# A decoder block on one core: SyncE's queue gets an order written out by hand, and 32 of 192 modulation rows move to the output projection

## The chip, the core and the metric

The kernel runs on one core of a Trainium2 chip. The core has TensorE (matrix products into PSUM), VectorE, ScalarE, GpSimd and SyncE, which here only issues DMA transfers. Each engine works through its own instructions in their order; between engines, semaphores say what has been done. The metric is the device time of one execution in microseconds. The kernel before takes 2344.61 us, the median of three runs from 2343.13 to 2346.32.

## The reference

One block on 512 tokens of width 2048, everything in float32:

```python
mod = c_act @ w_ada[l] + b_ada[l]
sh1, sc1, gt1, sh2, sc2, gt2 = jnp.split(mod[:, None, :], N_MOD, axis=-1)
h = _rmsnorm(x, norm1_g[l]) * (1.0 + sc1) + sh1
p = h @ w_in[l]
y_rwkv = _rwkv7_mixer(p[..., :N_RWKV_COLS], ...)
y_pool = _pool_mixer(p[..., N_RWKV_COLS:], ...)
mix = jnp.concatenate([y_rwkv, y_pool], axis=-1) @ w_out[l]
x = x + gt1 * mix
h = _rmsnorm(x, norm2_g[l]) * (1.0 + sc2) + sh2
x = x + gt2 * _conv_ffn(h, w_up[l], conv_w[l], conv_b[l], w_down[l])
return _rmsnorm(x, norm_f_g)
```

`_rwkv7_mixer` is a recurrence with a 64 x 64 state for each of 16 heads; its inputs r, k and v are 1024 columns each of `p`, its decay and gates come from three small low-rank products. `_pool_mixer` takes causal means over 2, 4, 8 and 16 tokens and a 256 x 256 product for each. The MLP has 5632 columns twice, with a causal convolution of width 3.

## The kernel before

Activations are kept transposed: 128 channels by 512 tokens in a tile. A float32 product is made of three faster ones: weights and activations are split into a rounded part and its remainder (`split_weights`: a load into `wraw`, a cast to `whi` on ScalarE, a subtraction to `wlo` on VectorE; `mm3`: three matmuls). `wraw` has four buffers, `whi` and `wlo` three each.

The stages are: the first norm and the first eight column tiles of the input projection (up to 156 us in the profile); the *recurrence* (163 to 761), in which the other 27 column tiles (`win_units`, L333) are interleaved with the recurrence and the pools; the output projection (761 to about 950), of which the first eight output tiles are made in whole rows of 512 tokens and the other eight in two halves of 256; the MLP; the last norm.

The recurrence treats two heads at a time, eight *pairs*. `stage_a` of a pair loads r, k and v and a small matrix `lw`, makes decays and scores, stores the 16 x 16 triangles of the scores to DRAM and loads them back in another layout (`dn`, `nl`), inverts them on VectorE in 14 doubling steps (`prod`, `xyl`, L466 to L475), and passes the result through DRAM again (`dx`, `x4w`, `x4`). `stage_b` does the chunked state update, and `post` the norm, the bonus and the gate, and stores the tile to `mixd` in DRAM, from which the output projection loads it. r, k and v of pair p are three column tiles of the projection; `win_pair` spills them to DRAM (`sp`), and `stage_a` loads them from there. One more load in this stretch are the modulation rows: 48 columns of `mod` are products of `c_act` with rows of `w_ada`, done on VectorE (`ada_rest`, L343 to L352) with the row in quarters: 4 x 48 = 192 loads of 256 KB into `war` (three buffers), each with one multiplication that sums along the row. `cq` holds the quarter of `c_act`. The other modulation rows are made before and after.

The loop `recurrence()` writes TensorE's order out by hand. It keeps a clock of its own, in us: one matmul of the projection adds 0.23, and each step of a stage yields what it takes and how long its next step must wait. Whenever no step is ready, a matmul of the projection is put in. Every sixth of these a modulation row follows. Inside `manual_schedule` TensorE's instructions stand in the order in which the loop emits them. Those of the other engines, SyncE's loads and stores too, are ordered by a scheduler, by priority and by when it thinks them ready.

Of the kernel before, what the change touches and what calls it, by code (L numbers as in the profile page):

```python
# [1 line left out]

# [26 lines left out]
NB = 10  # L29
NJ = NF // 2  # L30
# [27 lines left out]
def block_kernel(ctx, tc, a, out, stop=None, dbg=None):  # L58
# [52 lines left out]
    def split_weights(src, eng=V):  # L111
        raw = wp.tile([P, WC], F32, tag="wraw", name="wraw", bufs=4)
        nc.sync.dma_start(raw, src)
        hi = wp.tile([P, WC], F32R, tag="whi", name="whi", bufs=3)
        S.copy(hi, raw)  # L115
        lo = wp.tile([P, WC], F32R, tag="wlo", name="wlo", bufs=3)
        eng.tensor_tensor(lo, raw, hi[:, :].bitcast(F32), op=ALU.subtract)  # L117
        return hi, lo
# [7 lines left out]
    def project(ps, src, acts, start=True, stop=True, engs=(V,)):  # L126

        n = len(acts)
        for k0 in range(0, n, WC // P):
            wh, wl = split_weights(src[:, k0 * P : k0 * P + WC], engs[k0 // 4 % len(engs)])  # L130
# [48 lines left out]
    if True:  # L179
# [28 lines left out]
        for k in range(KT):  # L208
# [14 lines left out]
            for i0 in range(0, 8, WC // P):  # L223
                wh, wl = split_weights(a["win0"][k, :, i0 * P : i0 * P + WC])
# [8 lines left out]
        if True:  # L233
# [13 lines left out]
            S.activation(xwa[0:64, :], xwa[0:64, :], AF.Tanh)  # L247
            xg1 = ra.tile([P, T], F32, tag="xg1", name="xg1")
# [15 lines left out]
            upad = [ring16("upad") for i in range(2)]  # L264
            for i in range(2):
                V.memset(upad[i][:, 0:16], 0.0)
                S.copy(upad[i][:, 16:], pf[6 + i])
            ps0ctx.close()

    def load_pw(gi):  # L270
        t = ra.tile([P, T], F32, tag="war", name="pw", bufs=3)
# [24 lines left out]
    def pool_back(gi, zs, pw):  # L296
        for d in range(2):
# [6 lines left out]
            if gi:  # L304
                nc.sync.dma_start(mixd[8 + j], mx)
# [16 lines left out]

    def win_units(fi, ps):
# [16 lines left out]
    cq = [None]  # L340
    modq = ra.tile([P, 4, 48], F32, tag="modq", name="modq")

    def ada_rest(n0, n1):  # L343
        for n in range(n0, n1):
            kq, j = divmod(n, 48)
            if j == 0:
                cq[0] = ra.tile([P, T], F32, tag="cq", name="cq")
                nc.sync.dma_start(cq[0], cact[0:1, kq * T : (kq + 1) * T].partition_broadcast(P))
            wa = ra.tile([P, T], F32, tag="war", name="war", bufs=3)
            nc.sync.dma_start(wa, a["ada2"][kq, j, :, :])  # L350
            V.scalar_tensor_tensor(wa, wa, 1.0, cq[0], op0=ALU.mult, op1=ALU.mult,  # L351
                                   accum_out=modq[:, kq, j : j + 1])  # L352
# [16 lines left out]
    class Pair:  # L369
        begun = False  # L370

# [9 lines left out]
    def stage_a(p, q):  # L381
# [14 lines left out]
        yield 0.0, 4.0  # L396
# [15 lines left out]
        mid = ra.tile([P, NL, 1], F32, tag="mid", name="mid", bufs=2)  # L412
# [40 lines left out]
        nl = ra.tile([64, 16, 16], F32, tag="nl", name="nl")  # L453
        dn = tc.dram_tile([64, 16, 16], F32, name=f"dn{p}")
        for b in range(8):
            nc.sync.dma_start(dn[8 * b : 8 * b + 8, :, :].rearrange("s i j -> i s j"),
                              nt[16 * b : 16 * b + 16, :, 16 * (b % 4) : 16 * (b % 4) + 16])
        nc.sync.dma_start(nl, dn[:, :, :])
# [5 lines left out]
        V.scalar_tensor_tensor(k2, r, col("rk", p), k2, op0=ALU.mult, op1=ALU.mult)  # L464
        xyl = ra.tile([64, 2, 16, 16], F32, tag="xyl", name="xyl")
        V.tensor_add(xyl[:, 1, :, :], nl, lanei)  # L466
        prod = ra.tile([64, 64], F32, tag="prod", name="prod")
# [9 lines left out]
        nc.sync.dma_start(dx[:, :, :, :], xyl)  # L477
        for b in range(8):
            nc.sync.dma_start(x4w[16 * b : 16 * b + 16, :, :, 16 * (b % 4) : 16 * (b % 4) + 16],
# [254 lines left out]
    with tc.manual_schedule(engines={mybir.EngineType.PE}):  # L734
        recurrence()
# [606 lines left out]
```

## Time and profile before

One profiled execution took 2349.0 us; its span, from the first instruction to the last, is 2347.1 us, and the mean granted clock of TensorE 0.981.

| stretch, us | what | TensorE busy, us | VectorE busy, us | granted clock |
|---|---|---|---|---|
| 163 to 636 | recurrence up to the last pair's `stage_a` | 415.55 of 473 | 355.05 | 0.95 |
| 636 to 761 | rest of the recurrence | 121.56 of 125 | 69.61 | 0.99 |
| 761 to 852 | output projection, whole rows | 90.79 of 91 | 42.27 | 1.00 |
| 852 to 950 | output projection, half rows | 93.85 of 98 | 65.19 | 0.98 |

In rows of waits the first name is the engine and line that waited and the second what ended the wait; then total us, times and the longest. In rows of groups, the count, the busy us and mean ns of one, and the idle time of the engine before them. `SPq` is SyncE's queue. A row of transfers gives the count, the size and the median us from issue to landing.

### The profile page before, as it was taken

The page shows a single profiled execution, that of the slowest core. Times are in us where ns is not written, and L with a number is a line of the kernel's source. Part 1 is how long each engine was busy: PE and PEld are TensorE (multiplying, and loading weights), DVE is VectorE, ACT ScalarE, POOL GpSimd, SP SyncE. Part 2 cuts the span into 40 slices and gives each one's busy share as a digit, 9 for nine tenths or more (in the row PEclk, how much of TensorE's full clock was granted, in tenths as well). Part 3 has the DMA queues.
Part 4 walks back from the last instruction along what each step waited for, and adds up shares of the span by engine and source line. Part 5 has one row for each costly group of instructions (what it writes and reads, how often), then busy time and mean ns, then how long its engine had stood idle before and what let it go on. Part 6 is the DMA issues. An engine that isn't in the chain of part 4 may idle for free.

```text
span 2347.1 us, 42629 instructions
## 1 busy us (share of the span) xinstructions
PE 2206.0 (94%) x17090; PEld 1958.5 (83%) x17090; DVE 1611.8 (69%) x2543; ACT 1006.5 (43%) x1416; POOL 126.1 (5%) x183
## 2 busy tenths in 40 slices
PE   4778798898899999999999999999999999999997
PEld 3656566666677799999999999999999888888897
DVE  7977786877665366788888877777777645353454
ACT  3243333333333346655555555555555422233353
POOL 0000000000000010111010100000000000110000
PEclk9999899999999999999999999999999999999998
DMA  9966665666533766698888877777776667663464
GB/s 353 339 221 187 210 198 168 202 201 186 151 77 93 251 187 184 204 271 235 250 225 248 234 200 201 199 199 197 200 197 196 221 222 268 226 211 112 124 189 155
DMA packets 200218, 480.77 MB, mean 205 GB/s; under 512 B 46481, under 2 KB 53201, under 8 KB 191825
## 3 DMA queue, kind: packets, MB, share of 16 engines
q1 hardware_dynamic: 180098, 410.91, 53.7%
q0 software_dynamic: 18864, 66.07, 13.7%
q8 instruction: 134, 2.20, 0.4%
q10 hardware_dynamic: 1056, 1.05, 0.1%
q14 instruction: 66, 0.54, 0.1%
HBM read 440.45 MB, written 37.49 MB: 204 GB/s over the span
## 4 chain that ended last, share of the span: by engine, by line
PE 67%; DVE 12%; issue 11%; DMA 8%; ACT 2%; SPq 1%; POOL 0%; DVEq 0%; POOLq 0%; ACTq 0%
PE b L124 18%; PE b L122 18%; PE b L123 18%; PE mm L333 6%; DMA war<-ada 6%; DVE jk L214 3%; DVE war L351 2%; DVE wlo L117 1%; DMA wrow<-wup 1%; PE pa L300 1%; DVE sacc L199 0%; DVE al L151 0%; PE pb L570 0%; ACT ah L150 0%; DMA cq<-cact 0%
## 5 line engine op out<-in xcount | busy, mean ns | idle before, releaser
L124 PE MATMUL b<-t,ulo 128*128 128x256 f32 x1408 | 397.2, 282 | 0.0
L122 PE MATMUL b<-t,uhi 128*128 128x256 f32 x1408 | 396.8, 282 | 0.0
L123 PE MATMUL b<-t,uhi 128*128 128x256 f32 x1408 | 396.7, 282 | 0.0
L115 ACT CAST whi<-wraw 128x512 fp32r<-128x512 f32 x236 | 145.4, 618 | 381.9 <-PE mm L333 222.9
L124 PE MATMUL b<-act,ulo 128*128 128x512 f32 (+1 forms) x880 | 308.0, 350 | 0.0
L123 PE MATMUL b<-act,uhi 128*128 128x512 f32 (+1 forms) x880 | 307.8, 350 | 0.0
L122 PE MATMUL b<-act,uhi 128*128 128x512 f32 (+1 forms) x880 | 307.7, 350 | 0.0
L122 PE MATMUL b<-y,uhi 128*128 128x256 f32 x1056 | 298.1, 282 | 2.1 <-ACT uhi L930 2.1
L124 PE MATMUL b<-y,ulo 128*128 128x256 f32 x1056 | 297.8, 282 | 0.4 <-DVE ulo L932 0.4
L123 PE MATMUL b<-y,uhi 128*128 128x256 f32 x1056 | 297.9, 282 | 0.0
L932 DVE TENSOR_TENSOR ulo<-wd,uhi 128x1024 fp32r<-128x1024 f32 (+1 forms) x120 | 136.2, 1135 | 215.6 <-ACT uhi L930 210.8
L122 PEld LDWEIGHTS b<-t,uhi 128*128 128x128 f32 x1408 | 266.9, 190 | 0.0
L124 PEld LDWEIGHTS b<-t,ulo 128*128 128x128 f32 x1408 | 266.9, 190 | 0.0
L123 PEld LDWEIGHTS b<-t,uhi 128*128 128x128 f32 x1408 | 266.8, 190 | 0.0
L930 ACT CAST uhi<-wquart 128x1024 fp32r<-128x1024 f32 x156 | 163.8, 1050 | 203.8 <-PE b L123 177.5
L930 ACT CAST uhi<-wd 128x1024 fp32r<-128x1024 f32 (+1 forms) x120 | 117.3, 978 | 291.1 <-PE b L123 290.0
L932 DVE TENSOR_TENSOR ulo<-wquart,uhi 128x1024 fp32r<-128x1024 f32 x156 | 190.9, 1224 | 71.9 <-ACT uhi L930 71.9
L117 DVE TENSOR_TENSOR wlo<-wraw,whi 128x512 fp32r<-128x512 f32 x236 | 161.2, 686 | 82.3 <-ACT whi L115 81.5
L930 ACT CAST uhi<-r 128x1024 fp32r<-128x1024 f32 x132 | 138.6, 1050 | 162.8 <-PE b L123 159.2
L932 DVE TENSOR_TENSOR ulo<-r,uhi 128x1024 fp32r<-128x1024 f32 x132 | 161.2, 1222 | 61.8 <-ACT uhi L930 61.7
L122 PEld LDWEIGHTS b<-y,uhi 128*128 128x128 f32 x1056 | 200.2, 190 | 2.5 <-ACT uhi L930 2.5
L124 PEld LDWEIGHTS b<-y,ulo 128*128 128x128 f32 x1056 | 200.1, 190 | 0.6 <-DVE ulo L932 0.6
(302 smaller groups left out, 4455.7 us busy)
## 6 DMA issues: line engine op xcount, KB each, us to landing
wquart<-wup SPq DMA_DIRECT2D x176, 512.0 KB, 4.8
wa<-ada SPq DMA_DIRECT2D x48, 1024.0 KB, 6.9
war<-ada SPq DMA_DIRECT2D x192, 256.0 KB, 3.6
wd<-wdn SPq DMA_DIRECT2D x80, 512.0 KB, 4.0
wraw<-win SPq DMA_DIRECT2D x140, 256.0 KB, 4.2
wraw<-wout SPq DMA_DIRECT2D x96, 256.0 KB, 3.6
wquart<-wup POOLq DMA_DIRECT2D x44, 512.0 KB, 7.3
r<-wup SPq DMA_DIRECT2D x44, 512.0 KB, 4.5
```

The source lines that it names most:

```text
L115: S.copy(hi, raw)
L117: eng.tensor_tensor(lo, raw, hi[:, :].bitcast(F32), op=ALU.subtract)
L122: PE.matmul(ps, wh, xh, start=start, stop=False, skip_group_check=more)
L123: PE.matmul(ps, wh, xl, start=False, stop=False, skip_group_check=more)
L124: return PE.matmul(ps, wl, xh, start=False, stop=stop, skip_group_check=more)
L214: V.scalar_tensor_tensor(jk, wa, 1.0, cb, op0=ALU.mult, op1=ALU.mult, accum_out=mod[:, j : j + 1])
L300: PE.matmul(ps, pw[:, i, d * P : (d + 1) * P], zs[i], start=i == 0, stop=i == 1)
L333: PE.matmul(ps, w[:, sl], x, start=k == 0 and i == 0, stop=k == KT - 1 and i == 2)
L351: V.scalar_tensor_tensor(wa, wa, 1.0, cq[0], op0=ALU.mult, op1=ALU.mult, accum_out=modq[:, kq, j : j + 1])
L930: S.copy(hi[:, 0:n], src)
L932: lo_of[0] = V.tensor_tensor(lo[:, 0:n], src, hi[:, 0:n].bitcast(F32), op=ALU.subtract)
```

## The change

SyncE joins TensorE under the order of the loop. So each load and store in the recurrence stands where the loop emits it, and the loop now says when:

- Weight blocks of the projection are loaded three blocks before their split (`load_block`, `blocks`), and modulation rows three rows ahead (`AHEAD`, `load_ada`, four buffers). `cq` is loaded when its last row has been used, and three row slots go by before the next row.
- Stores that follow a chain are put on a list with a due time (`defer`) and emitted when the clock reaches it: the spill of r, k, v after 3.0 us, which also is what lets `stage_a` begin, `mixd` after 2.0 or 3.0, `dx` 24 us after the load of `nl`, `x4w` 3 us later. `stage_a` gets a step of its own for `dn` and for `nl`.
- `upad` is read from PSUM earlier. The last pool weights lie in another buffer, `mid` has one buffer, `prod` is smaller.
- 40 of the 48 modulation columns are made in the recurrence (160 rows), and eight (32 rows) in the output projection: after each of its output tiles, one row is loaded through the `wraw` buffers and multiplied (`ada_last`).

```diff
+    def load_block(i):
+        if i < 27 * 4:
+            blocks.append(load_weights(a["win1"][i // 4, :, i % 4 * WC : (i % 4 + 1) * WC]))
+    def defer(us, fn):
+        late.append((clock[0] + us, len(late), fn))
     def win_units(fi, ps):
-        src = a["win1"][fi - 8, :, :]
         for k0 in range(0, KT, WC // P):
-            wh, wl = split_weights(src[:, k0 * P : k0 * P + WC])
+            wh, wl = split_weights(blocks.pop(0))
             for kk in range(WC // P):
+                if kk == 1:
+                    load_block((fi - 8) * 4 + k0 // 4 + 3)
...
+    def load_ada(n):
+        if n < 4 * NQ:
+            t = ra.tile([P, T], F32, tag="war", name="war", bufs=4)
+            nc.sync.dma_start(t, a["ada2"][n // NQ, n % NQ, :, :])
+            was.append(t)
+    def ada(n):
+        kq, j = divmod(n, NQ)
+        wa = was.pop(0)
+        V.scalar_tensor_tensor(wa, wa, 1.0, cqs[kq], op0=ALU.mult, op1=ALU.mult, accum_out=modq[:, kq, j : j + 1])
+        load_ada(n + AHEAD)
+        if j == NQ - 1 and kq < 3:
+            load_cq(kq + 1)
...
+        defer(INV, lambda: nc.sync.dma_start(dx[:, :, :, :], xyl))
+        defer(INV + 3.0, spread)
...
+    def spill(p, i, t):
+        nc.sync.dma_start(sp[p, i], t)
+        if i == 2:
+            made.add(p)
...
-            d = tc.dram_tile([P, T], F32, name=f"sp{p}_{i}")
-            nc.sync.dma_start(d, t)
-            sp[p, i] = d
-        made.add(p)
+            sp[p, i] = tc.dram_tile([P, T], F32, name=f"sp{p}_{i}")
+            defer(3.0, partial(spill, p, i, t))
...
+            due = [t for t in late if t[0] <= clock[0]]
+            for t in sorted(due, key=lambda t: t[:2]):
+                late.remove(t)
+                with hp():
+                    t[2]()
...
-    with tc.manual_schedule(engines={mybir.EngineType.PE}):
+    with tc.manual_schedule(engines={mybir.EngineType.PE, mybir.EngineType.SP}):
         recurrence()
...
+    def ada_last():
+        for kq in range(4):
+            if kq % 2 == 0:
+                cq2 = wide("cq2").rearrange("p a b -> p (a b)")
+                nc.sync.dma_start(cq2, cact[0:1, kq * T : (kq + 2) * T].partition_broadcast(P))
+            for j in range(48 - NQ):
+                wa = load_weights(a["ada2"][kq, NQ + j, :, :])
+                V.scalar_tensor_tensor(wa, wa, 1.0, cq2[:, kq % 2 * T : (kq % 2 + 1) * T], op0=ALU.mult, op1=ALU.mult,
+                                       accum_out=modr[:, kq, j : j + 1])
+                yield
+        mod_done(modr, NQ, 48)
+        yield
```

More of the change, by code (lines that the diff above doesn't have):

```diff
@@ L29 @@
 NB = 10
+AHEAD = 3
+NQ = 40
+INV = 24.0
 NJ = NF // 2
@@ L339, in block_kernel, with load_cq @@
     G.memset(x4w, 0.0)
[L340 to L352, printed above, removed]
+    modq = ra.tile([P, 4, NQ], F32, tag="modq", name="modq")
+    cqs, was = [], []
+    def load_cq(kq):
+        t = ra.tile([P, T], F32, tag="cq", name="cq", bufs=1)
+        nc.sync.dma_start(t, cact[0:1, kq * T : (kq + 1) * T].partition_broadcast(P))
+        cqs.append(t)
+    def load_ada(n):
[10 more added lines that the diff above has]
+            load_cq(kq + 1)
     HS = (slice(0, 64), slice(64, 128))
@@ L882, in block_kernel @@
         out_half(0, f)
+        next(adas)
+    next(adas)
     steps = first_half()
```

108 lines of the change are left out of this document (69 added, 39 removed).

## The prediction

> **What bounds the kernel now.** I read the page first (span, busy shares, chain that ended last), then the busy time by stretch, then the waits of TensorE and of VectorE in the stretch that is not full, then SyncE's queue there.
>
> ```profile
> span 2347.1 us, 42629 instructions
> ...
> PE 67%; DVE 12%; issue 11%; DMA 8%; ACT 2%; SPq 1%; POOL 0%; DVEq 0%; POOLq 0%; ACTq 0%
> ```
>
> This line of the chain says that TensorE carries two thirds of it, but that VectorE and DMA have a fifth. Where that fifth lies is read from the stretches (columns: stretch, length, then busy time of PE, PEld, DVE, ACT, POOL; granted clock; DMA share; GB/s). 163 is the first matmul of L333, 636 the first matmuls of the last pair's `stage_a`, 761 the end of the recurrence, 852 the start of the output projection's half rows.
>
> ```profile
> 163.00:636.00 473.00, 415.55 (x4212) 312.70 (x4212) 355.05 (x944) 160.88 (x249) 0.00 (x0) 0.95 0.63 189
> 636.00:761.00 125.00, 121.56 (x1269) 91.44 (x1269) 69.61 (x153) 44.50 (x71) 0.00 (x0) 0.99 0.33 91
> 761.00:852.00 91.00, 90.79 (x393) 73.52 (x393) 42.27 (x64) 34.50 (x56) 3.95 (x7) 1.00 0.67 220
> 852.00:950.00 98.00, 93.85 (x763) 93.16 (x763) 65.19 (x106) 58.44 (x101) 8.64 (x16) 0.98 0.61 183
> ```
>
> From 163 to 636 TensorE lacks 473.0 - 415.6 = 57.4 us, and the clock lacks 0.05 x 473 = 24 us. After 636, where the modulation rows are nearly done, it lacks 3.4 us, and the output projection is full. So what can be won lies in the first stretch. Its waits, of VectorE and then of TensorE (total, times, longest):
>
> ```profile
> DVE war L351 <- DMA war<-ada: 70.1, 59, 3.7
> ...
> DVE war L351 <- DMA cq<-cact: 6.7, 3, 4.0
> ```
> ```profile
> PE pb L563 <- DVE Tm L560: 15.4, 4, 6.5
> PE pb L601 <- DVE rw L602: 8.7, 9, 1.7
> PE mm L333 <- DVE wlo L117: 8.1, 3, 4.7
> PE pa L426 <- ACT sq L395: 8.0, 1, 8.0
> ```
>
> TensorE waits for small VectorE steps, and VectorE, which works in order, has sat in front of them waiting for modulation rows: 76.8 of its 473 - 355 = 118 idle us. One such place:
>
> ```profile
> 393.84 0.69 DVE L351 SCALAR_TENSOR_TENSOR war<-war,cq 128x512 f32<-128x512 f32 x1 [4.01 <-DMA cq<-cact]
> ...
> 395.68 0.68 DVE L560 TENSOR_TENSOR Tm<-pb,mlev 128x512 f32<-128x512 f32 x1
> ```
>
> Behind the first row stands `Tm` of L560, whose delay is the 6.5 us wait above.
>
> **The change part by part.** Costs of the rows (count, busy, mean ns, idle before), and landings in the same stretch (count, size, median us):
>
> ```profile
> L351 DVE SCALAR_TENSOR_TENSOR war<-war,cq 128x512 f32<-128x512 f32 x188 | 127.1, 686 | 77.4 <-DMA war<-ada 70.1 <-DMA cq<-cact 6.7
> ...
> L236 DVE SCALAR_TENSOR_TENSOR spill<-mm,vec,spill 128x511 f32<-128x511 f32 x21 | 15.6, 741 | 0.2 <-ACT spill L235 0.2
> L351 DVE DVE_READ_ACCUMULATOR war<-war,cq 128x1 f32 x188 | 15.2, 81 | 0.0
> ```
> ```profile
> war<-ada SPq DMA_DIRECT2D x186, 256.0 KB, 3.6
> ...
> sp<-spill SPq DMA_DIRECT2D x21, 256.0 KB, 3.5
> ...
> dn<-sb SPq DMA_DIRECT2D x56, 8.0 KB, 1.9
> ...
> lw<-lora SPq DMA_DIRECT2D x7, 64.0 KB, 3.4
> ```
>
> *Rows loaded three ahead, in order (AHEAD, four buffers).* A row is used every sixth matmul of L333; a buffer freed by one row is needed four rows later. At the loop's 0.23 us per matmul that is 4 x 6 x 0.23 = 5.5 us, against 3.6 us landing: 1.9 us are spare, so with SyncE on time the 70.1 us go. SyncE will not always be on time: in the fixed order it stops for the landing of a `dn` store (1.9), of `dx` (3 us of clock later) and of the spilled `v` (3.5), each pair. Three stops a pair, each some 1.5 to 2 us more than what is spare, over seven pairs: 30 to 40 us of row waits stay, about half of 77. Bounds: none stay, all stay.
>
> *32 rows fewer here.* By this point 188 rows had run; the new loop does 160 by then and none later. 28 x (0.686 + 0.081) = 21 us of VectorE work less. VectorE had 118 idle us against TensorE's 57; now it gets 42 + 21 = 63 us more room. I take two thirds of the 57.4 us of TensorE gaps as gone: -38 (bounds -57, all of them, and -10, what the rows alone might give). What is late next: the short steps of L601, 1 to 2 us each, which have other causes too.
>
> *The clock.* Half clock follows gaps. A gap and the stretch after it:
>
> ```profile
> 446.50 1.22 PE L426 MATMUL pa<-sq,hmat 128*128 128x512 f32 x1 [2.92 <-DVE Tm L535]
> 446.40:449.80 3.40, 3.30 (x12) 1.62 (x14) 2.90 (x9) 1.95 (x5) 0.00 (x0) 0.50 0.37 112
> ```
>
> A 2.92 us gap was followed by 3.4 us at 0.50, 1.7 us lost. Of the 24 us a part lies in the gaps themselves and costs nothing; with two thirds of the gaps gone I take -12 (bounds 0 and -20).
>
> *`v`, then `lw`, in a fixed place.* Before, `rkv` and `lw` were loaded as soon as they could be. SyncE's queue at pair 4:
>
> ```profile
> 437.93 0.33 SPq L648 DMA_DIRECT2D sp<-spill  x1
> ...
> 441.30 0.33 SPq L387 DMA_DIRECT2D v<-sp  x1
> ...
> 442.20 0.38 SPq L393 DMA_DIRECT2D lw<-lora  x1
> ```
> ```profile
> 510.58 0.69 PE L401 MATMUL pa<-xwa,lw 64*128 64x512 f32 x1
> ```
>
> The `lw` at 442.20 is that of pair 5, whose matmul came 68 us later. In the new order the store of the third spill, `r`, `k`, `v`, `lw` stand together, and the first matmul of `stage_a` reads `lw`. Let the tile's last matmul end at 0. The shift on ScalarE and VectorE takes about 1.7 us (0.74 for L236, the like for ScalarE, and hops: an estimate from that row), the store's wait in front of `v` 441.30 - 437.93 = 3.4, `lw` 0.4 later, landing 3.4: 8.9 us. TensorE reaches that matmul at 3.0 (the deferral) + 4.0 (the yield) + about 0.3 = 7.3. It waits 1.6 us, more where VectorE or SyncE is late: I take 2.5 for pairs 2 to 5, 1 for pairs 6 and 7, whose start lies 2 to 3 us later in the loop: +12, and +3 of half clock as after the 2.92 us gap. Bounds: 0 (a short landing, TensorE late elsewhere) and 7 x (1.6 + 3.7) = +37, with the longest wait for a row in front of the shift. The Trainium skill ("TensorE: Matmul & The Clock Gate", "HAM oscillation") says that the half clock comes after gaps above about 3.4 us. By it the +3 would be nothing and the sum below -30; the 2.92 us row speaks against it. While SyncE stands before `v`, rows and weight blocks wait behind it; three weight blocks are already loaded, so the rows alone feel it, counted above.
>
> *Chain stores, `dx` at 24 us, the earlier `upad`, pool weights, `prod`, `mid`:* same instructions at other places, 0. The earlier `upad` frees banks sooner, but weights now stand behind `cq` and three rows in the queue: 0, bounds -5 and +3.
>
> *32 rows in the output projection.* They are VectorE work under a full TensorE: 32 x 0.77 = 25 us in 42.3 + 65.2 busy of 189: hidden. But they take turns with `wout` in the four `wraw` buffers. Rates and landings there:
>
> ```profile
> 780.00:800.00 20.00, 20.00 (x90) 16.57 (x89) 5.47 (x8) 5.04 (x9) 0.00 (x0) 1.00 0.94 336
> 860.00:880.00 20.00, 20.00 (x169) 20.00 (x168) 12.15 (x20) 9.70 (x17) 1.62 (x3) 1.00 0.69 208
> ```
> ```profile
> x<-xT SPq DMA_DIRECT2D x2, 1024.0 KB, 7.6
> wraw<-wout SPq DMA_DIRECT2D x3, 256.0 KB, 5.5
> ```
> ```profile
> wraw<-wout SPq DMA_DIRECT2D x38, 256.0 KB, 3.7
> ```
> ```profile
> L115 ACT CAST whi<-wraw 128x512 fp32r<-128x512 f32 x88 | 54.3, 619 | 71.1 <-PE b L123 30.6 <-PE pa L123 9.5 <-PE pb L123 9.0
> L117 DVE TENSOR_TENSOR wlo<-wraw,whi 128x512 fp32r<-128x512 f32 x88 | 60.4, 690 | 54.5 <-ACT whi L115 53.9
> ```
>
> The landings are those of 785 to 800 (first two) and of 840 to 900. Twelve matmuls take 12 x 20/90 = 2.67 us for a whole block, 12 x 20/169 = 1.42 for a half. A buffer's turn is landing + 0.62 + 0.69 + 0.1: 5.1 us at 3.7, 6.9 at 5.5. Whole blocks: it now comes back every two blocks, 5.3 us, before every four. At 3.7 it just holds, at 5.5 it costs 0.8 a block. Half rows: five loads for 5.7 us in four buffers, 5/4 x 5.1 = 6.4, so 0.7 x 8 = 5.6 us. Casts stand up to two blocks ahead, which swallows some 4 us. The first eight blocks also ask for 16 x 0.262 + 4 x 1.05 + 0.52 = 8.9 MB in 21.4 us, 26.5 us at the 336 GB/s of that row. I take half of the 24 whole blocks at 0.8 and the half rows, less the lead: 9.6 + 5.6 - 4 = 11; the half rows begin with such a lead again, some 3 more: +8. Bounds 0 and +42 (below).
>
> Sum: -38 - 12 + 12 + 3 + 8 = -27. The profiled execution took 2349.0 us (span 2347.1), 4.4 above the median 2344.61 of the three runs; so 2322 for it, and 2318 as the median.
>
> **The rivals.** *The ring starves the output projection (slower).* If landings there are 5.5 throughout, 24 x 0.8 = 19 and 8 x (5/4 x 6.9 - 5.7) = 23 us: +42 instead of +8, and the sum is +7: 2352. It decides from a landing of about 5.2 us on, where the cost passes the 35 won before. For it: 5.5 in the row above, with 1 MB loads in the queue. Against: 3.7 in the longer stretch. The Trainium skill ("DMA: Bandwidth & Descriptors", "Where 436 GB/s comes from") puts one core's HBM limit at about 358 GB/s; by it the first eight blocks would need 24.9 us, not 26.5, and this rival would be 2 us cheaper; the row shows 336.
>
> *SyncE's stops give the waits back (no change).* If 55 to 60 of the 77 us stay because stops in front of `v`, `dx` and `dn` eat the lead, the gaps shrink by 20 and the clock by 5, against +23: about 2343. For it: the stops are those of the queue's own rows below, in which it could still put other loads between.
>
> ```profile
> SPq L387 <- DMA sp<-spill: 14.1, 17, 2.0
> ...
> SPq L479 <- DMA dx<-xyl: 6.4, 6, 2.6
> ```
>
> Against: these two sum to 20.5 us only, and 1.9 us of each stop are spare.
>
> *Nearly everything goes.* Rows never late, `lw` in time: -50 - 18 + 3 + 4 = -61: 2284. For it: the 3.4 us lacking after 636. Against: VectorE is then 85% busy, (355 - 21) of the 0.95 x 415.6 = 395 us that TensorE needs at full clock.
>
> **How the numbers follow.** 0.2% is 4.7 us, about what three runs that spread over 3.2 us can tell. Forecast (2300 to 2335) 0.54, nearly everything (below 2300) 0.16, no change (2335 to 2349) 0.15, starving 0.15. The predicted time is 2318. 80%: 2288 to 2351; the likeliest's own range is 2300 to 2335. Faster 0.54 + 0.16 + 0.06 = 0.76; the rest of "no change" with it 0.09 same; 0.15 slower.
>
> **What would show it.** VectorE's wait for `war<-ada` between the first matmul of the recurrence and `stage_a` of pair 7: 30 to 40 us, before 70.1; TensorE's gaps there about 35 with the new ones; a new wait of the `lw` matmuls (L432) on DMA, four to six times, 1 to 4 us each; the recurrence about 35 us shorter; `whi` waiting for `wraw` in the output projection, which gets 5 to 12 us longer; from the gated MLP on nothing. It is wrong if `war` waits stay above 55, if the output projection grows by over 25, or if L432 waits over 5 us a pair.

## The result, and the profile after

The changed kernel takes 2365.51 us (median of four runs, 2364.01 to 2369.13) where the kernel before takes 2343.87 beside it: ratio 1.0094, 95% interval 1.0076 to 1.0111. It is slower, by 21.6 us; the prediction was 2318, with 2288 to 2351 as its range. The profiled execution took 2364.73 us, 15.7 more than that of before. The two differences are not the same because the profiled execution of before, 2349.0 us, lies 5 us above its median, and that of the changed kernel 1 us below.

The page of the changed kernel, first line and chain:

```profile
span 2363.0 us, 42509 instructions
...
PE 60%; DMA 13%; DVE 11%; issue 10%; ACT 3%; SPq 2%; POOL 0%; ACTq 0%; POOLq 0%; DVEq 0%
```

The chain now lies on DMA for 13% where it was 8, and on TensorE for 60 where it was 67. The stretches of the changed kernel (columns as before):

```profile
162.00:637.60 475.60, 420.01 (x4241) 316.53 (x4241) 337.28 (x890) 163.24 (x254) 0.00 (x0) 0.95 0.57 171
637.60:753.00 115.40, 113.19 (x1238) 85.08 (x1238) 64.78 (x141) 40.49 (x65) 0.00 (x0) 1.00 0.33 94
753.00:858.00 105.00, 97.02 (x398) 74.22 (x396) 55.09 (x111) 34.49 (x56) 2.66 (x5) 0.97 0.76 250
858.00:966.60 108.60, 99.11 (x775) 94.49 (x775) 72.55 (x132) 58.63 (x105) 9.94 (x19) 1.00 0.64 196
```

TensorE's gaps in the first stretch are 475.60 - 420.01 = 55.6 us; they were 57.4. The recurrence as a whole, from the first matmul of the loop to the first of the output projection, went from 598.0 to 591.0 us. The whole rows of the output projection went from 91.0 to 105.0 and the half rows from 99.4 to 108.5: 23 us lost there. Everything behind them differs by less than 2 us a stage.

Waits of the changed kernel between 162 and 637.6: VectorE, then TensorE, then ScalarE, then SyncE's queue.

```profile
DVE war L379 <- DMA war<-ada: 36.8, 30, 4.6
DVE wlo L124 <- ACT whi L122: 32.4, 21, 5.3
...
DVE war L379 <- DMA cq<-cact: 4.4, 1, 4.4
```
```profile
PE mm L355 <- DVE wlo L124: 12.1, 2, 8.8
PE pb L645 <- DVE rw L646: 11.6, 9, 2.3
PE pa L432 <- DMA lw<-lora: 11.3, 5, 3.7
PE mm L355 <- DVE v L243: 6.0, 1, 6.0
PE pb L607 <- DVE Tm L604: 4.3, 3, 1.8
```
```profile
ACT whi L122 <- DMA wraw<-win: 93.8, 26, 8.1
ACT whi L122 <- PE mm L355: 73.1, 26, 9.4
```
```profile
SPq L373 <- DVE war L379: 39.9, 26, 8.6
SPq L495 <- DVE sb L481: 33.1, 5, 7.4
SPq L680 <- DVE rs L679: 32.4, 4, 15.4
SPq L686 <- DVE spill L243: 26.7, 5, 11.3
SPq L686 <- DVE rw L646: 22.1, 3, 11.0
SPq L686 <- DVE prod L509: 20.9, 4, 6.7
```

VectorE's wait for rows fell from 76.8 to 41.2 us. In its place VectorE waits 32.4 us for `whi`, and ScalarE 93.8 us for weight blocks. The same rows of before read:

```profile
DVE wlo L117 <- ACT whi L115: 7.8, 9, 1.8
```
```profile
ACT whi L115 <- DMA wraw<-win: 2.6, 1, 2.6
```
```profile
war<-ada SPq DMA_DIRECT2D x186, 256.0 KB, 3.6
wraw<-win SPq DMA_DIRECT2D x83, 256.0 KB, 4.0
```

SyncE, in its fixed order, stands in front of stores (`dn` L495, `mixd` L680, the spill L686) until VectorE has made their data, up to 15.4 us at a time, and weight blocks and rows stand behind them. They also take longer to land than in the rows of before just shown, although less is moved in the mean (171 GB/s, before 189):

```profile
war<-ada SPq DMA_DIRECT2D x155, 256.0 KB, 4.7
wraw<-win SPq DMA_DIRECT2D x84, 256.0 KB, 4.9
```

A row's load follows the one before it at 1.2 us in the median and 3.0 in the mean; before, it was 1.9 and 2.6. So the loads now go out in bunches between SyncE's stops. That the bunches make the landings longer is likely, but no run shows it.

The row waits of these two views, between 163 and 640, can be sorted by when the load had been issued (the n-th load in the trace belongs to the n-th multiplication). Before, 32 of them (42 us) were of rows issued over 1 us after their buffer came free, and 27 (28 us) of rows issued at once. After, the first kind stands at 25 (33 us) and the second at 5 (3 us). So loading three rows ahead removed most of the waits that it can remove, and waits of rows that were issued late stayed. (The expectation of e5 below counts a few more, with the same picture.)

### The profile page after: what moved, and what is told of

Same layout as the page of the kernel before. It is cut to its first block, busy times and chain, and to the rows that moved or that the text cites. A ratio compares the mean times of both kernels' runs of the same rounds, so it can differ in the third digit from the quotient of the medians.

```text
span 2363.0 us, 42509 instructions
## 1 busy us (share of the span) xinstructions
PE 2211.2 (94%) x17090; PEld 1960.0 (83%) x17090; DVE 1608.8 (68%) x2548; ACT 1003.9 (42%) x1414; POOL 126.1 (5%) x183
## 4 chain that ended last, share of the span: by engine, by line
PE 60%; DMA 13%; DVE 11%; issue 10%; ACT 3%; SPq 2%; POOL 0%; ACTq 0%; POOLq 0%; DVEq 0%
PE b L129 17%; PE b L131 17%; PE b L130 17%; PE mm L355 5%; DMA wraw<-wout 3%; DMA war<-ada 3%; DVE jk L221 2%; DMA wraw<-win 2%; DVE wlo L124 2%; DVE war L379 1%; DMA wrow<-wup 1%; SPq L495 1%; ACT whi L122 1%; DMA sp<-spill 1%; PE pa L310 1%
```

## The experiments

All numbers of a stage are read from one profile of each kernel, from the start of its first matmul to that of the next stage's; differences under some 4 us are not weighed. The executions of one kernel spread over 2 to 12 us, so a difference of about 10 us has to be read beside the ratio, which comes from medians of all executions: 0.1% is 2.3 us. Gaps are the length less TensorE's busy time. "Lost clock" is half the length of the spells at a granted clock of 0.50. Ratios are to the kernel before on the same chip, in brackets their 95% interval.

| kernel | recurrence, us | gaps | lost clock | whole rows | half rows | ratio |
|---|---|---|---|---|---|---|
| before | 598.0 | 60.8 | 27.3 | 91.0 | 99.4 | 1 |
| changed | 591.0 | 57.6 | 21.3 | 105.0 | 108.5 | 1.0094 [1.0076, 1.0111] |
| e1_stores_pool | 579.4 | 52.3 | 16.2 | 105.2 | 109.0 | 1.0066 [1.0051, 1.0081] |
| e2_no_move | 597.2 | 62.2 | 24.6 | 93.2 | 99.4 | 1.0038 [1.0027, 1.0049] |
| e3_own_ring | 593.7 | 57.6 | 28.0 | 100.0 | 107.6 | 1.0069 [1.0054, 1.0084] |
| e4_lw_first | 583.9 | 55.5 | 17.4 | 106.1 | 113.3 | 1.0062 [1.0043, 1.0082] |
| e5_sp_free | 580.5 | 47.4 | 20.4 | 104.0 | 111.8 | 1.0016 [1.0005, 1.0028] |
| e6_before_no_rows | 547.3 | 26.4 | 4.9 | 91.2 | 99.4 | 0.9815 [0.9798, 0.9831] |
| e7_chain_pool | 619.2 | 80.3 | 34.7 | 105.4 | 109.6 | 1.0231 [1.0209, 1.0253] |
| e8_no_row_loads | 550.5 | 29.6 | 5.8 | 95.5 | 99.4 | 0.9826 [0.9812, 0.9841] |
| e9_before_rows_pool | 637.3 | 92.4 | 32.8 | 91.3 | 97.9 | 1.0144 [1.0123, 1.0166] |
| e10_rows_pool | 598.2 | 61.6 | 29.4 | 104.2 | 111.8 | 1.0123 [1.0110, 1.0137] |
| e11_no_row_waits | 581.2 | 47.6 | 21.1 | 100.7 | 107.8 | 0.9995 [0.9983, 1.0006] |
| e12_mix | 582.7 | 52.1 | 19.3 | 93.6 | 100.0 | 0.9946 [0.9933, 0.9960] |
| e13_quarter_rows | 561.7 | 38.4 | 11.0 | 99.3 | 102.4 | 0.9878 [0.9857, 0.9898] |
| e14_before_no_waits | 601.2 | 65.9 | 30.6 | 91.1 | 99.4 | 1.0043 [1.0029, 1.0058] |
| e15_before_quarter | 571.4 | 39.0 | 17.0 | 91.8 | 98.8 | 0.9894 [0.9872, 0.9917] |
| e16_mix_free | 582.7 | 48.3 | 22.4 | 92.4 | 100.9 | 0.9956 [0.9940, 0.9971] |
| e17_mix_free_pool | 581.8 | 54.9 | 12.2 | 93.1 | 100.9 | 0.9978 [0.9967, 0.9990] |
| e18_paced | 587.0 | 53.2 | 23.5 | 92.4 | 98.2 | 0.9967 [0.9955, 0.9980] |

In every kernel the length of the recurrence less the two columns behind it is 504 to 516 us. So TensorE's gaps and its clock account for most of what differs, and the question is what makes the gaps.

### The parts of the change, undone one at a time

**e1_stores_pool.** Spill and `mixd` stores leave SyncE's queue.

```diff
-        nc.sync.dma_start(sp[p, i], t)
+        nc.gpsimd.dma_start(sp[p, i], t)
```
(and the same for both stores to `mixd`)

> The changed kernel with the chain stores in the recurrence (the spills of r, k, v and the `mixd` tiles) issued from GpSimd's queue, so that SyncE no longer stops in front of them. Theory 1 (SyncE, in its fixed order, stops before stores whose data VectorE has not made, and weight blocks behind them come late: ScalarE waits 93.8 us for `wraw<-win`): that wait falls below 40 us, TensorE's gaps between 162 and 638 fall from 55.6 to about 30, and the recurrence is 20 to 35 us shorter than in the changed kernel, about 560 us. Theory 3 (VectorE works in order with little to spare, and TensorE waits for VectorE's own splits and short steps; loads that come late only fill its slack): ScalarE's wait for weight blocks falls too, but the recurrence gets at most 8 us shorter and TensorE's gaps stay above 45.

In the profiled execution, the fastest of its four, the recurrence is 11.6 us shorter. By the ratios the kernel gained 0.28%, some 7 us, which is far less than theory 1 said and does not exclude theory 3. ScalarE's wait for weights fell to 56.4 us only. SyncE's queue in this run, 163 to 637:

```profile
SPq L495 <- DVE sb L481: 65.9, 7, 18.2
SPq L373 <- DVE war L379: 51.5, 31, 9.5
SPq L418 <- DMA sp<-spill: 48.3, 6, 14.6
```

With some stops removed, SyncE arrives earlier at the next ones: `dn` from 33.1 to 65.9 us, the landing of the spills from 10.8 to 48.3.

**e4_lw_first.** `lw` is loaded ahead of r, k and v.

```diff
     def stage_a(p, q):
+        lw = ra.tile([P, P], F32, tag="lw", name="lw")
+        nc.sync.dma_start(lw, a["lora"][p, :, 0, :])
...
-        lw = ra.tile([P, P], F32, tag="lw", name="lw")
-        nc.sync.dma_start(lw, a["lora"][p, :, 0, :])
```

> The changed kernel with `lw` loaded at the head of `stage_a`, ahead of r, k and v, so that it does not stand behind the landing of the spilled `v`. If the new wait of the `lw` matmuls is a cost of its own (the prediction's +12, measured 11.3): it falls below 2 us and the recurrence of 591.0 us gets 8 to 14 us shorter. If another chain ends at the same time (r and k are also late there, and so `sq` on ScalarE): the wait is gone but TensorE waits for `sq` or a later step of the same stage, and the recurrence stays within 4 us of 591.

The wait of L432 for `lw`, 11.3 us, is no longer among TensorE's waits, and the recurrence is 7.1 us shorter: between the two expectations, nearer the first. The ratios say the same, 0.32% or 7.5 us.

**e5_sp_free.** TensorE alone in the written order.

```diff
-    with tc.manual_schedule(engines={mybir.EngineType.PE, mybir.EngineType.SP}):
+    with tc.manual_schedule(engines={mybir.EngineType.PE}):
```

> The changed kernel with TensorE alone in the written order: SyncE's loads and stores in the recurrence are ordered by the scheduler again; the loads ahead, the four row buffers and the deferred stores stay in the code. If the written order of SyncE is what keeps the row waits alive (rows issued late behind stops: 27 of 35 waits, 35.7 of 39.3 us), and the deeper buffers are what removed the others: the recurrence falls below 575 us (591.0), VectorE's row waits below 25 us, ScalarE's wait for `wraw<-win` below 30. If the scheduler, too, puts stores and weight loads that must wait ahead of rows (in the kernel before a row was issued late in 32 of 63 waits): the recurrence stays between 580 and 598.

The written order of SyncE costs 10.5 us of recurrence (591.0 against 580.5) in the two profiles and 0.8% of the whole, some 18 us, by the medians; the profiled execution of e5 is 5 us above its median. A second pair with this one difference, e2 and e16 below, gives 14.5 us and again 0.8%. ScalarE's `whi` waits 0.6 us for weight blocks, as expected, yet VectorE's waits for rows stay, where 25 us had been expected as the most (161 to 638):

```profile
DVE war L379 <- DMA war<-ada: 38.5, 34, 3.7
```

Only 17 us of them (12 of 34) are now of rows issued late. At 580.5 us the recurrence lies between the two cases.

**e2_no_move** and **e3_own_ring**: the moved rows.

```diff
-NQ = 40
+NQ = 48
```
(and no `ada_last`: e2)
```diff
-                wa = load_weights(a["ada2"][kq, NQ + j, :, :])
+                wa = rb.tile([P, 2, 4, HT], F32, tag=f"y{j % 4}", name="adar")[:, 0, 0:2, :].rearrange("p a b -> p (a b)")
+                nc.sync.dma_start(wa, a["ada2"][kq, NQ + j, :, :])
```
(e3)

> The changed kernel with all 192 rows made in the recurrence, none in the output projection. If the rows in the ring of four `wraw` buffers are what lengthened the output projection: its whole rows go back from 105.0 to about 91 us, its half rows from 108.5 to about 99. The recurrence: by the prediction's reckoning 28 rows more of VectorE work, 21 us, of which a third lies under TensorE's waits: 0 to 8 us longer than in the changed kernel. Sum -24 + 4: about 2345 us, level with the kernel before. If instead something else of the change (where loads stand when the output projection begins) lengthened it, it stays above 195 in all, and the time above 2355.

> The changed kernel with the 32 rows of the output projection loaded into four buffers of their own (tiles that are not in use yet), weights alone in the `wraw` buffers. If the turn of the ring is what costs: whole and half rows take about 94 and 101 us, 18 us less than in the changed kernel, about 2347 us. If the bytes (whole rows already at 250 GB/s, 336 at the most) or the order of SyncE's queue cost it: the same 213 us within 6, about 2365 us.

With the rows back in the recurrence the output projection takes 192.6 us instead of 213.5, as expected, and the recurrence 6.2 more. Buffers of their own win back only 5.9 of these 20.9 us: the turn of the `wraw` ring is a quarter of the cost. In e3 VectorE waits for rows instead, `ah` for `mxl`, and rows take 5.7 us to land (waits and transfers, 754.8 to 854.8):

```profile
DVE adar L906 <- DMA adar<-ada: 22.6, 13, 3.5
ACT ah L150 <- DMA mxl<-mixd: 18.2, 6, 6.0
```
```profile
adar<-ada SPq DMA_DIRECT2D x32, 256.0 KB, 5.7
wraw<-wout SPq DMA_DIRECT2D x30, 256.0 KB, 4.2
```

All 32 rows are loaded during the whole rows there, and the half rows, with no row left to load, are still 8.2 us longer than before. Their first 30 us have 5.6 us of gaps and lose 1.7 of clock, where before had nothing of either: they begin without the lead that the splits had.

### What a row costs in the recurrence, and by what

**e6_before_no_rows** and **e8_no_row_loads**: each kernel without its row loads.

```diff
-            nc.sync.dma_start(wa, a["ada2"][kq, j, :, :])
-            V.scalar_tensor_tensor(wa, wa, 1.0, cq[0], op0=ALU.mult, op1=ALU.mult,
+            V.scalar_tensor_tensor(wa, xg1, 1.0, cq[0], op0=ALU.mult, op1=ALU.mult,
```
(e6; e8 does the same in `load_ada` and `ada` and, with `cq2`, in `ada_last`)

> The kernel before with the 192 loads of modulation rows left out (the multiplications run on a tile that is already in SBUF, so the modulation columns 32 to 79 are wrong; that part of the computation is left out). It gives the price of the 76.8 us that VectorE waits for rows there. The prediction's view (these waits are what delays the short steps that TensorE waits for): TensorE's gaps in 163 to 636 fall from 57.4 to about 20 and the time by 45 to 55 us, to about 2295. Theory 3 (the waits lie mostly where VectorE had room): gaps stay above 40, and the time falls by 5 to 20 us.

> The changed kernel with all 192 loads of modulation rows left out; the multiplications stay and run on tiles already in SBUF, so the modulation columns 32 to 79 are wrong and that part of the computation is left out. Output projection: if the loads of the rows (bytes and places in the queue) lengthened it, 192 us in all instead of 213.5; if VectorE's 32 multiplications did, above 205. Recurrence: the kernel before without these loads took 547.3 us. If the fixed order costs only through the rows, the same here, 545 to 555; if SyncE's stops delay the weight blocks by themselves (theory 1), 560 to 575, with ScalarE's wait for `wraw<-win` still above 40 us.

Before, the loads cost 50.7 us of recurrence, as the prediction's view had it (1.85% or 43 us by the medians). In the changed kernel they cost 40.5. The recurrence multiplies 189 rows before and 157 after, so a row costs 0.27 us before and 0.26 after: the change made the rows fewer, not cheaper. Without them the two kernels are 3.2 us apart, although SyncE still stops before stores and ScalarE still waits 54.8 us for weights in e8: the written order costs next to nothing where no rows are in the queue, so theory 1 as it stood (the stops alone make the loss) falls. In the output projection the loads are 18.6 of the 23 us; VectorE's multiplications 2 to 5. Of e8, ScalarE and SyncE between 161 and 638, and the weight blocks' landing:

```profile
ACT whi L122 <- DMA wraw<-win: 54.8, 17, 6.2
```
```profile
SPq L685 <- DVE spill L243: 67.1, 8, 15.5
SPq L679 <- DVE rs L678: 53.1, 6, 17.3
```
```profile
wraw<-win SPq DMA_DIRECT2D x95, 256.0 KB, 3.9
```

**e11_no_row_waits** and **e14_before_no_waits**: the loads stay, VectorE no longer waits for them.

```diff
-        V.scalar_tensor_tensor(wa, wa, 1.0, cqs[kq], ...
+        V.scalar_tensor_tensor(rowout, xg1, 1.0, xg1, ...
```
(e11; e14 the same in the kernel before, with one line more)
```diff
+            G.tensor_tensor(modq[:, kq, j : j + 1], wa[:, 0:1], modq[:, kq, j : j + 1], op=ALU.add)
```

> Two edits, read in two stages; both leave work out (modulation columns 32 to 79 are wrong). Recurrence: the row loads stay in SyncE's order with their bytes, but the multiplications read a tile that is always in SBUF (no load of `cq` either), so VectorE never waits for a row. If VectorE's waits for rows are the price: the recurrence goes to 550 to 558 us, as without the loads (550.5). If the rows cost by what they do to the weight blocks behind them (ScalarE waits 93.8 us for `wraw<-win`, without rows 54.8): 570 to 585. Output projection: the 32 loads stay in the `wraw` buffers but bring a quarter of each row (64 KB), VectorE's work stays. If the bytes are what costs: 194 to 200 us in all (213.5; without the loads 194.9). If the turns in the ring and the places in the queue cost it: above 207.

> The kernel before with its row loads kept, but the multiplications read a tile that is always in SBUF (no `cq`), so that VectorE never waits for a row; GpSimd reads one column of the row after the multiplication, which keeps the buffer until then. Modulation columns 32 to 79 are wrong. If VectorE's 76.8 us of waits for rows were what made TensorE's gaps there (the prediction's -38 and -12): the recurrence falls from 598.0 to 550 to 565 us. If they were only the place where VectorE's idle time showed, and the loads cost through the weight blocks and the chains' own loads: 580 to 595.

This is the test of the prediction's main step. Without any wait of VectorE for a row, the changed kernel's recurrence is 9.8 us shorter, of the 40.5 that the loads cost; by the medians e11 is 23 us faster, of which 5.0 are in the output projection, so at most some 18. In the kernel before the recurrence is not shorter at all. There SyncE stands in front of row loads as long as ever, 165 us in e14 beside 176 before (all rows of L347 and of L350 together), and the chains' own loads come late behind it. First SyncE in before, then SyncE and VectorE in e14 (161 to 638):

```profile
SPq L350 <- DVE war L351: 90.6, 80, 5.9
```
```profile
SPq L347 <- DMA war<-ada: 101.3, 76, 3.7
SPq L347 <- POOL modq L350: 63.9, 115, 4.2
```
```profile
DVE xyl L464 <- DMA nl<-dn: 25.5, 5, 10.4
```

Because of this, e14 says that taking the wait from VectorE alone is worth nothing. It doesn't say what VectorE's waits would cost if SyncE's stops for a free buffer went with them, and its GpSimd reads add two waits of VectorE of their own, 8.3 and 3.0 us. Both runs also leave out the loads of `cq`, as do e13 and e15.

**e13_quarter_rows** and **e15_before_quarter**: places and waits stay, a quarter of the bytes.

```diff
-            nc.sync.dma_start(t, a["ada2"][n // NQ, n % NQ, :, :])
+            nc.sync.dma_start(t[:, 0:P], a["ada2"][n // NQ, n % NQ, :, 0:P])
```
(without `cq`; the multiplication reads `wa[:, None, 0:P].to_broadcast([P, 4, P])`; in e13 the rows of the output projection likewise, in the buffers of e3)

> The changed kernel with a quarter of each modulation row loaded (64 KB instead of 256) and used four times over, so that the multiplication has its length; the places in the queues and the waits stay, no `cq` in the recurrence, and in the output projection the rows have buffers of their own. Modulation columns 32 to 79 are wrong. If the bytes of the rows are what costs (they take the DMA engines from the weight blocks: 4.9 us landings, 3.9 without rows): the recurrence goes to 550 to 562 us (591.0; without the loads 550.5). If the places in SyncE's queue cost it, stops in front of rows and rows behind stops: 575 to 590. Output projection: own buffers alone gave 207.6 us, a quarter of the bytes alone 208.5; if both ring and landing limit it, both edits give 194 to 199; if neither does (order in the queue), above 204.

> The kernel before with a quarter of each row loaded (64 KB) and used four times over, no `cq`; places in the queue, waits and VectorE's work stay. Modulation columns 32 to 79 are wrong. If the bytes are the price of the rows in the recurrence (598.0 us with them, 547.3 without): 550 to 562. If it is their places in SyncE's queue and their turn in three buffers: 575 to 590.

In the changed kernel a quarter of the bytes took away 29.3 of the 40.5 us that the loads cost, in the kernel before 26.6 of 50.7. Transfers in the recurrence of e13:

```profile
wraw<-win SPq DMA_DIRECT2D x104, 256.0 KB, 3.8
war<-ada SPq DMA_DIRECT2D x155, 64.0 KB, 3.1
```

Weight blocks, whose size is unchanged, land in 3.8 us instead of 4.9. SyncE's stops before stores are still there (42.1 us at L680, 38.6 at L495 between 161 and 638), and so are VectorE's waits for rows:

```profile
DVE rowout L378 <- DMA war<-ada: 40.9, 28, 6.0
```

In the changed kernel, then, the waits stayed as long as they were (36.8 and 4.4 for `cq`) and most of the price went: there the bytes cost, and not through the length of VectorE's waits. In the kernel before it can't be told apart, for in e15 VectorE's waits fell with the bytes, from 76.8 to 40.4 us. By the medians the quarter rows are worth 25 us of 43 before, and 51 of 63 after with the output projection. What is left in the recurrence, 24 us before and 11 after, is the quarter of the bytes that is still loaded, the places in the queues and VectorE's waits together; no run separates these.

In the output projection the quarter rows win 5.0 us in the ring (e11) and 11.8 in buffers of their own (e13), of 18.6: ring and bytes add up there, and 7 us belong to neither.

**e7_chain_pool, e9_before_rows_pool, e10_rows_pool**: other queues. e7 takes every chain transfer to GpSimd's queue, e9 and e10 the rows, in the kernel before and in the changed one.

```diff
-            nc.sync.dma_start(wa, a["ada2"][kq, j, :, :])
+            nc.gpsimd.dma_start(wa, a["ada2"][kq, j, :, :])
```
(e9)

> The changed kernel with every transfer of the recurrence's chains (spill, r, k, v, `lw`, `dn`, `nl`, `dx`, `x4w`, `mixd`) issued from GpSimd's queue; SyncE keeps only weight blocks, modulation rows and `cq`, in their fixed order, and stops there for a free buffer alone. Theory 1 (stops in the fixed queue are what holds weights and rows back; with only the first three kinds of stores moved, SyncE had stopped in front of `dn`, 65.9 us, and of the landing of the spills, 48.3 us, instead): ScalarE's wait for `wraw<-win` below 15 us, VectorE's for `war<-ada` below 20, recurrence 550 to 562 us (591.0 in the changed kernel, 579.4 with the stores moved). Theory 2 (the landings of 4.7 to 4.9 us, that is the traffic, make them late): both waits stay above 35 us and the recurrence above 575. Theory 3 (VectorE's own order): the waits go but the recurrence stays above 575.

> The kernel before with the 192 row loads issued from GpSimd's queue, which has nothing else to do in the recurrence, instead of SyncE's. Theory 1 (a row is late because its load stands behind others in SyncE's queue: up to 10 us passed there between a buffer coming free and its load being issued): VectorE's wait for rows falls from 76.8 to below 30 us and the recurrence from 598.0 to 560 to 575, about 2310 us. Theory 2 (a row is late because three buffers and a landing of 3.6 us leave no lead): the wait stays above 55 us and the recurrence within 8 us of 598.

> The changed kernel with the loads of the modulation rows of the recurrence issued from GpSimd's queue, where they wait for their own buffer alone; all else stays in SyncE's written order. If late issue behind other entries of SyncE's queue is the cause of the row waits that are left: they fall from 41 us to below 15, TensorE's gaps from 57.6 to about 40 and the recurrence to 565 to 577 us. In the kernel before the same move made things worse (recurrence 598.0 to 637.3 us, row waits 77 to 108), with three buffers and with no lead; if that came from GpSimd's queue as such and not from the missing lead, the recurrence is above 600 here too.

All three are slower than the kernel that they change; the gains that their first cases expected did not come. The Trainium skill ("DMA: Bandwidth & Descriptors", "Issuing engines are not separate DMA queues") says that transfers issued from different engines run on the same 16 DMA engines, so that spreading them gives no bandwidth. The trace of e10 agrees: it moves 168 GB/s between 161 and 638, where the changed kernel moves 171. A row lands in 4.1 us there instead of 4.7, but r and k, which stayed in SyncE's queue, in 6.6 instead of 3.8, and the recurrence is 7 us longer. In e10 only one or two of the 40 row waits are of rows issued late, as wanted, and VectorE waits 46.1 us for rows all the same: its rows follow one another at 1.25 us in the median (2.7 in the mean), and the fourth buffer is asked for 5.3 us after it came free, of which the landing takes 4. In e7 ScalarE's wait for weights is 6.6 us, as expected, and that for rows grew; SyncE now stops for `wraw` buffers, with rows behind (161 to 638, SyncE and VectorE):

```profile
SPq L117 <- DVE wlo L124: 220.3, 45, 15.7
```
```profile
DVE war L379 <- DMA war<-ada: 85.9, 53, 5.5
```

VectorE waits for a row that stands behind a weight load in SyncE's queue, and this load waits for a `wlo` that stands behind that row in VectorE's. The scheduler's order of VectorE also changed in these three, which isn't separated; why e9 lost 39 us stays open.

### Mixes

**e12_mix** is e1, e2 and e4 together. **e16_mix_free** is e2 and e5 together, **e17_mix_free_pool** adds the stores of e1, **e18_paced** is e16 with the rows asked for by the loop's clock:

```diff
-                        if n % 6 == 0:
+            if clock[0] >= row:
+                row += 2.55
```

> A candidate: the changed kernel with all rows in the recurrence, the chain stores from GpSimd's queue, and `lw` at the head of `stage_a`. From the single edits: recurrence 591.0 + 6.2 - 11.6 - 7.1 = 578.5 us, output projection 192.6, so 34 us less than the changed kernel and about 16 less than the kernel before: 2325 us, ratio 0.993. If the three edits remove the same waits (each frees SyncE for the same loads), half of it: 2340, level with the kernel before.

> The changed kernel with SyncE ordered by the scheduler and all 192 rows in the recurrence: what is left of the change is the row buffers and loads ahead, the deferred stores and the small steps. From the single edits: recurrence 580.5 + 6.2 = 587, output projection 192.6, so 2343.6 - 11 - 2 = 2331 us, ratio 0.995. If without the written order the extra 28 rows cost what a row costs on average ((591.0 - 550.5) / 160 = 0.25 us each): the same within 2 us. If the two interact (28 rows more at once, row waits above 55 us): 2340 and above.

> SyncE ordered by the scheduler, all 192 rows in the recurrence, and the chain stores (spills and `mixd`) from GpSimd's queue. If a scheduled SyncE already goes around the stops before these stores (their waits there: 14.3 and 7.3 us, in the written order 85.8 and 32.4): the recurrence stays at 582.7 us within 4, the time at ratio 0.996. If they cost the same in both orders: 571 us, ratio 0.991.

> SyncE ordered by the scheduler, all 192 rows in the recurrence, and the rows asked for by the loop's clock, one every 2.55 us over the whole recurrence (before: one every sixth matmul of the projection, 1.4 to 3.3 us apart, the last at 475 of the loop's 525 us). Same bytes, same places in the queue, an even rate. If the rate in the dense stretches is what makes landings long (4.0 us for a row, 4.1 for a weight block): both fall to about 3.7, TensorE's gaps from 48 to about 40, and the recurrence from 582.7 to 568 to 576 us, ratio 0.990 to 0.993. If the bytes cost wherever they lie: 580 to 587, and part of the lost time moves behind 636 us.

e12 and e16 are faster than the kernel before, by 0.54% and 0.44%, near the sums expected for them (0.7% and 0.5%). In e17 the stores from GpSimd's queue bring nothing once SyncE is scheduled, as its first case had it. e18 is inconclusive: 186 rows are loaded between 161 and 638 as in e16, at 1.5 us in the median beside 1.3, so the even pace of 2.55 us was never there; the recurrence is 4 us longer.

From e16 the parts of the change can be read one after the other in the recurrence: loads ahead, deeper buffers and the small steps 598.0 to 582.7; the moved rows to 580.5 (e5); the written order of SyncE to 591.0. In the output projection the moved rows add 22.5 us between e16 and e5. For the whole kernel the medians give -0.44% for the first part, +0.60% for the moved rows and +0.78% for the written order.

## Why the prediction was wrong

- *Where the time is.* Right: only the recurrence and the output projection moved.
- *Rows three ahead.* Right in size: 30 to 40 us of row waits were said to stay, 41.2 did. With SyncE on time all were to go; in e5, where the scheduler orders SyncE, 42.5 stayed as well, and 22 of its 34 waits for `war<-ada` were of rows issued at once. The stops were named too narrowly. I counted SyncE's stops for landings (L418, L518); the long ones are before stores whose data VectorE hasn't made, which I had costed at 0 under "chain stores".
- *"I take two thirds of the 57.4 us of TensorE gaps as gone: -38."* This is the step that failed. The gaps of the stretch fell by 1.8 us; without the 11.3 of the new `lw` wait, by 13. The step took VectorE's waits for rows as the cause of the gaps because they were the largest entry among VectorE's waits, and let two thirds of the gaps go with half of the waits. Without any row load (e6) the gaps of the recurrence fall from 60.8 to 26.4, by 34.4 us: even all the rows' loads together did not carry 38. In size the loads did cost what I had put on them, 50.7 us beside -38 and -12, but with their bytes and places. In the changed kernel it isn't mainly VectorE's wait that costs: without it (e11) 9.8 us of 40.5 went, and with the waits in place and a quarter of the bytes (e13) 29.3. In the kernel before, e14 speaks against the wait, and e15 can't part it from the bytes. The change left 160 of 192 rows with all their bytes, nearly all in this stretch, so the lateness stayed and showed as waits for `whi`, `wraw` and `lw`.
- *32 rows fewer.* I set the 188 rows inside the stretch before against all 160 after; within the recurrence it is 189 against 157, 32 fewer, so the term should have been 32 x 0.767 = 25 us. VectorE's busy time there fell by 23 us; by e16 and e5 this is worth 2 us.
- *The clock.* -12 and +3 forecast; -6.0 measured, though the gaps that were to carry it stayed.
- *`lw` after `v`, +12.* Right: 11.3 us, five times, 3.7 the longest; undoing it gave 7.1.
- *32 rows in the output projection, +8.* Mis-sized: 23 measured, 20.9 when undone, inside the bounds of 0 and 42. I had let four us of the splits' lead stand against the cost; instead the lead was used up, and 18.6 us are the loads. The place:

```profile
793.00:803.00 10.00, 9.32 (x40) 7.11 (x39) 3.90 (x9) 1.54 (x4) 0.00 (x0) 1.00 0.96 339
803.00:813.00 10.00, 4.24 (x13) 3.00 (x12) 5.31 (x10) 3.56 (x6) 0.00 (x0) 0.66 0.87 302
813.00:823.00 10.00, 10.00 (x46) 8.14 (x45) 6.51 (x12) 4.39 (x6) 0.00 (x0) 1.00 0.98 342
```
```profile
ACT whi L122 <- DMA wraw<-wout: 36.8, 18, 4.5
...
PE pb L129 <- ACT whi L122: 6.8, 2, 5.8
```

  At 803 TensorE stops for 5.8 us and loses clock behind it, with the DMA engines at 0.87 to 0.98 and 302 to 342 GB/s. The Trainium skill ("DMA: Bandwidth & Descriptors", "Where 436 GB/s comes from") gives about 358 GB/s for a core. These slices stay below it, but it is no limit in these traces: between 20 and 40 us the kernel before moves 417 GB/s.
- *The rivals.* Starvation needed landings of 5.2 us; they were 4.2 in the whole rows and 3.7 in the half rows, so the stage is the one that this rival named, but the cost came without its slow landings. "SyncE's stops give the waits back" named the cause of 10.5 us (e5; 18 by the medians), but with row waits of 55 to 60.
- *What would have shown it wrong.* None of the three signs that I gave came (rows above 55, output projection over 25, `lw` over 5): they tested the waits, and not the step from the waits to the gaps. The forecast that did test it, gaps of about 35 us, failed with 55.6.

The account, profile to profile: -27 was forecast. The gaps without `lw` came out 25 higher (-13 for -38), the clock 3 (-6 for -9), `lw` 1 lower, the output projection 15 higher (23 for 8): +15. Measured: +15.7. By the medians it was +21.6, and the 6 us between the two can't be given to a stage.

Open: what the remaining 11 (after) and 24 us (before) of the rows' price are, what VectorE's waits cost in the kernel before, and by which of the late transfers the bytes act. A kernel in which VectorE, too, has a written order wasn't tried.

## What to carry to other kernels

The largest wait on an engine is not the price of that wait: where in-order queues hang together, lateness is passed on, and only an experiment that leaves the work, the wait or the bytes out one at a time tells which of them costs. A written order for a DMA queue must count every store in it as a stop until its data are made, with all loads behind. Here an order that can go around such stops won 0.8% (e5), another queue for the stores 0.3% (e1), and with the scheduled order nothing more (e17). Work moved under a full engine still has to pass the DMA engines there, and it uses up the lead of what it stands among.

## What the runs showed of the hardware

- Bytes cost far below the rate seen elsewhere. The first stretch of the changed kernel moves 171 GB/s in the mean, half of the 342 above (291 in the busiest of 40 slices), with the DMA engines at 0.57. Yet with a quarter of the rows' bytes weight blocks land in 3.8 us instead of 4.9.
- A queue of its own for the rows won nothing: issued from GpSimd, at 101.0 / 188 = 0.54 us of GpSimd each, a row landed in 3.4 us where SyncE's took 3.6 (e9 and before), and the recurrence was 39 us longer.
- Lost clock grew faster than gaps from e6 to before: 26.4 us of gaps lost 4.9 us of clock, 60.8 lost 27.3. It isn't set by their sum alone, for e17 with 54.9 us of gaps lost 12.2.
- The half clock also came after gaps well below the 3.4 us that the prediction quotes. The two spells of it in the recurrence of e6, 3.4 us each at 252.8 and 413.2, follow gaps of 1.9 us, the longest in the 7 us before them. All spells of before and of the changed kernel there last 3.4, 6.8 or 10.2 us.
